# Lower parts of the weights all on VectorE, and attention units that follow their own columns of queries

## The chip, the cores and the metric

One core of a Trainium2 chip runs the program. The time is device microseconds of one execution; a time given for a kernel is the median of several. The engines are TensorE (PE; its weight loads PEld), VectorE (DVE), ScalarE (ACT), GpSimd (POOL) and SyncE (SP, which here only issues transfers).

## The reference

One decoder layer on 256 tokens of width 2048, all in float32, cut to what matters:

```python
xn = rms_norm(h, attn_norm_w)
nq, kcmp, vcmp, kslc, vslc, kwin, vwin, ngate, fq, fk, fv, ff = split(xn @ w_in)
# NSA, 16 heads in groups of 4 that share keys: three branches, gated
kc, vc = compress_blocks(kcmp), compress_blocks(vcmp)      # 15 blocks
p_cmp  = masked_softmax(nq @ kc * scale + bias_c)
o_nsa  = g0 * (p_cmp @ vc) + g1 * selected(nq, kslc, vslc) + g2 * window(nq, kwin, vwin)
# FoX, 16 heads: causal attention with a forgetting bias c[t] - c[s]
o_fox  = masked_softmax(fq @ fk * scale + c_t - c_s) @ fv
h = h + concat(rms_norm(o_nsa), rms_norm(o_fox)) @ w_out
# MoE: 4 groups x 8 experts, 2 of them for each token
h = h + sum_e combine[:, e] * ((silu(hn @ w_gate[e]) * (hn @ w_up[e])) @ w_down[e])
return rms_norm(h, final_norm_w)
```

With 256 tokens the selected and the window branch both see all causal keys.

## The kernel before

**Items.** The weights of w_in and w_out stream through SBUF in pieces of 1 MB, called items, in one fixed order. Items 0 to 3 are the compressed keys and values (kcv), 4 and 5 v0, 6 and 7 k0, 8 and 9 v1, 10 and 11 k1. The NSA queries come in four blocks of 256 columns, two items each: q00 (12, 13), q01 (14, 15), q10 (16, 17), q11 (18, 19); the first digit is the group G of 8 heads, the second the half i. FoX follows: fq00, fq01 (20 to 23), fk00 (24, 25), fv00 (26, 27), fk01 (28, 29), fv01 (30, 31), and the same for G = 1 in 32 to 43. Items 44 to 59 are w_out. `run_items` (L235) does an item: it issues a load three items ahead, converts the next item's two halves (`stream_conv`, L178), runs the matmuls, and calls `background` (L225) after each quarter. Items 4 to 43 have 8 pieces of 128 rows (nk = 8), the others 4.

**Conversion.** A float32 weight is split into an upper and a lower part. ScalarE copies the upper part (L191), then a subtraction makes the lower part (L192). For items of nk = 8 the first half's subtraction is on VectorE and the second half's on GpSimd (L189). The two halves rotate through three buffers (L185), so a half is converted when TensorE is done with the half three before it. A projection's matmuls use both parts, and the result is evacuated by ScalarE and VectorE (`end`, L320).

**Background work.** Each call of `background` moves on one step of the attention pipe (`attn_pipe`, L205) and one step of the generators in `misc` and in `splits`. The pipe takes four steps for a unit: step 1 computes scores and softmax of a new unit (`a`), step 2 transposes the probabilities of the one before it (`b`), step 4 multiplies that one by its values (`c`). So one item is one unit, and its `b` and `c` run in the next item. NSA has 16 units (`Tile`, L640): for a pair of heads first the tile of 256 keys (t = 1), then the one of 128 (t = 0), whose `c` ends the pair in `pair_end` (L572). There the compressed branch is added, by a matmul with `pTc[G]`. FoX has 8 units (`Unit`, L586), one for a pair of heads.

**Queries and the compressed part.** When a query block is done, `post_q` (L788) evacuates it into `scaled`, splits it into parts for the scores (`split_q`, L709: for i = 0 at once, for i = 1 in a step of `misc`), and appends `compressed(G, q, i)` (L730) to `misc`. That makes the scores with the compressed keys (csc), a softmax on VectorE and ScalarE with two clamps of 8 elements (L752, L758), and writes half of `pcm`. With i = 1, four steps later, it transposes `pcm` into the bank bpt (L772) and copies it to `pTc[G]`. The eight NSA units of a group are appended after its second block, so at items 15 and 19: they start in items 16 and 24, and the first FoX units in item 32.

**Banks.** csc, bpt, the scores (s_n, s_f) and the transposes (t_n, t_f) all take their PSUM bank from one tag `s` with three buffers in rotation (L96). A new one waits for the last reader of the one three before it.

**Other GpSimd work.** In the same stretch GpSimd adds the position parts for the compressed keys (bk, L500, eight additions in items 8 and 9, which the matmuls bhc need), the causal mask to the FoX bias (L822, L823, when a FoX bias is loaded) and the squares of the attention output (L580 to L584).

**Experts.** A ring of 20 slots holds expert weights. Two slots are loaded once 16 units are finished (L1116), others as w_out moves on (`at2`, L1137), and all later ones when the experts have used a slot.

Of the kernel before, what the change touches and what calls it, by code (L numbers as in the profile page):

```python
# [11 lines left out]
F32 = mybir.dt.float32  # L12
# [4 lines left out]
ALU = mybir.AluOpType  # L17
# [4 lines left out]
P = 128  # L22
T = 256
# [3 lines left out]
NBLK = 15  # L27
# [53 lines left out]
def tile_kernel(ctx: ExitStack, tc: tile.TileContext, a: dict, out):  # L81
    nc = tc.nc
    pe, act, dve, pool, sp = nc.tensor, nc.scalar, nc.vector, nc.gpsimd, nc.sync
# [12 lines left out]
    def bank(name, tag):  # L96
        return psa.tile([P, 512], F32, tag=tag, name=name, bufs=1 if tag == "o" else 3)
# [9 lines left out]
    with tc.using_default_side("right"):  # L107
        fp = rt_st.enter_context(tc.tile_pool(name="fp", bufs=1))
        wk = rt_st.enter_context(tc.tile_pool(name="wk", bufs=2))
        ap_q = rt_st.enter_context(tc.tile_pool(name="ap_q", bufs=2))  # L110

    def m8(tag, name, shape, dt=F32):
        return big.tile([P, *shape], dt, tag=tag, name=name)

    def mm(o, l, r, start, stop):
        pe.matmul(o, l, r, start=start, stop=stop, skip_group_check=True)  # L116
# [17 lines left out]
    ident = cst[:, K_ID:K_ID + P]  # L134
# [43 lines left out]
    def stream_conv(h):  # L178

        i, hf = divmod(h, 2)  # L180
        if i >= len(items):
            return
        nm, _, nk = items[i][:3]
        n2 = nk // 2
        cv = big.tile([P, n2, 2, 2048 // nk], F32R, tag=f"c{h % 3}", name=f"cv_{nm}_{hf}")  # L185
        hi, lo = cv[:, :, 0, :], cv[:, :, 1, :]
        r = raws[i][:, n2 * hf:n2 * hf + n2, :]
        n = n2 if h else n2 // 2
        eng = pool if hf and nk == 8 else dve  # L189
        for k in range(0, n2, n):  # L190
            act.activation(hi[:, k:k + n], r[:, k:k + n], AF.Copy)  # L191
            eng.tensor_tensor(lo[:, k:k + n], r[:, k:k + n], hi[:, k:k + n].bitcast(F32), ALU.subtract)  # L192
        halves[h] = cv

    def run_chunk(i, kk):
# [5 lines left out]
    misc, splits = deque(), deque()  # L201
# [33 lines left out]
    def run_items(lo_i, hi_i, after=None):  # L235
        for i in range(lo_i, hi_i):
            nk, post = items[i][2], items[i][4]
            stream_dma(i + DMA_AHEAD)
            for kk in range(nk):
                if kk % (nk // 2) == 0:  # L240
                    stream_conv(2 * i + 2 + 2 * kk // nk)
                run_chunk(i, kk)
                if (kk + 1) % (nk // 4) == 0:
                    background()
            if post is not None:
                post()
            if after is not None:
                after(i)
# [236 lines left out]
    vcbd = []  # L485
# [86 lines left out]
    def pair_end(i, oT):  # L572

        if i < 8:
            G, j = divmod(i, 4)
            mm(oT[:, :T], vcbd[0][:, G, j, :], pTc[G], False, True)
        act.copy(oraw[i // 8][:, i % 8, :], oT[:, :T])
        part = i // 8
        if i % 8 == 0:
            pool.tensor_tensor(sq[:, part, :], oraw[i // 8][:, i % 8, :], oraw[i // 8][:, i % 8, :], ALU.mult)  # L580
        else:
            s2 = wk.tile([P, T], F32, tag="s2", name=f"s2_{i}", bufs=1)
            pool.tensor_tensor(s2, oraw[i // 8][:, i % 8, :], oraw[i // 8][:, i % 8, :], ALU.mult)
            pool.tensor_tensor(sq[:, part, :], sq[:, part, :], s2, ALU.add)  # L584
# [121 lines left out]
    def evac_q(s_, q, i):  # L706
        row_scale(q[:, 2 * i:2 * i + 2, :], s_, 0.125)

    def split_q(s_, qs, j):  # L709

        act.copy(qs[0:64, j:j + 2, 0, :], s_[0:64, j:j + 2, :])
        dve.tensor_tensor(qs[64:128, j:j + 2, 0, :], s_[0:64, j:j + 2, :], qs[0:64, j:j + 2, 0, :].bitcast(F32),
                          ALU.subtract)
        u = qs[64:128, j:j + 2, 1, :]
        act.copy(u, s_[64:128, j:j + 2, :])
        act.copy(qs[0:64, j:j + 2, 1, :], u.bitcast(F32))
        dve.tensor_tensor(u, s_[64:128, j:j + 2, :], u.bitcast(F32), ALU.subtract)

    def split_q_later(q, qs):
        yield  # L720
        split_q(q, qs, 2)
        yield

    pTc = {}
    gb = gate.rearrange("p t (h b) -> p h t b", b=3)
    biases = {}

    pcms = {}

    def compressed(G, q, i):  # L730

        csc = bank(f"csc{G}{i}", "s")
        for t in range(2):
            for r in range(2):
                o0 = (t * 2 + r) * 32
                mm(csc[:, o0:o0 + 32], q[:, 2 * i + r, t * P:(t + 1) * P],
                   kcd[:, 2 * G + i].rearrange("p h c -> p (h c)"), t == 0 and r == 0, True)
        yield
        if i == 0:
            pcms[G] = wk.tile([P, 2, P], F32, tag="pcm", name=f"pcm{G}", bufs=1)  # L740
            pool.memset(pcms[G], 0.0)
        scs = wk.tile([P, 8, 16], F32, tag="scs", name=f"scs{G}{i}", bufs=2)
        mx = wk.tile([P, 8], F32, tag="mx", name=f"mx{G}{i}", bufs=2)
        ss = wk.tile([P, 8], F32, tag="ss", name=f"ss{G}{i}", bufs=2)
        scv = scs[:, :, 0:NBLK]
        for t in range(2):
            dve.tensor_tensor(scv[:, 4 * t:4 * t + 4],
                              csc[:, 64 * t:64 * t + 64].rearrange("p (u c) -> p u c", c=16)[:, :, 0:NBLK],
                              cb[:, t, 4 * G + 2 * i:4 * G + 2 * i + 2].rearrange("p r h c -> p (r h) c")[:, :, 0:NBLK],
                              ALU.add)  # L750
        dve.tensor_reduce(mx, scv, AX.X, ALU.max)
        dve.tensor_scalar(mx, mx, -1e29, None, ALU.max)  # L752
        dve.tensor_tensor(scv, scv, mx.unsqueeze(2).broadcast_to([P, 8, NBLK]), ALU.subtract)
        yield
        act.activation(scv, scv, AF.Exp)
        yield
        dve.tensor_reduce(ss, scv, AX.X, ALU.add)
        dve.tensor_scalar(ss, ss, 1e-30, None, ALU.max)  # L758
        dve.reciprocal(ss, ss)
        sst = ss.rearrange("p (t h) -> p t h", t=2)  # L760
        dve.tensor_tensor(sst, sst, gate.rearrange("p t (h b) -> p t h b", b=3)[:, :, 8 * G + 4 * i:8 * G + 4 * i + 4, 0],
                          ALU.mult)
        for t in range(2):
            dve.tensor_tensor(pcms[G][:, t, 64 * i:64 * i + 64].rearrange("p (h c) -> p h c", c=16)[:, :, 0:NBLK],
                              scv[:, 4 * t:4 * t + 4], sst[:, t].unsqueeze(2).broadcast_to([P, 4, NBLK]), ALU.mult)
        if i == 0:
            return
        for _ in range(4):
            yield
        bpt = bank(f"bpt{G}", "s")  # L770
        for t in range(2):
            pe.transpose(bpt[:, t * P:(t + 1) * P], pcms[G][:, t], ident)  # L772
        pt = fp.tile([P, T], F32, name=f"pTc{G}")
        act.copy(pt, bpt[:, :T])
        pTc[G] = pt
        yield

    def nsa_bias(g):
        if g not in biases:
            bias = ap_q.tile([P, 4, T], F32, tag="m6", name=f"bias{g}", bufs=2)  # L780
            act.dma_start(bias, bass.AP(tensor=rv_dr.tensor, offset=rv_dr.offset + 4 * g * 384,
                                        ap=[[1, P], [384, 4], [1, T]]))
            biases[g] = bias
        return biases[g]
# [3 lines left out]
    def post_q(s_, G, i):  # L788
        q = scaled
        evac_q(s_, q, i)  # L790
        if i == 0:
            qs2[G] = m8(f"m{2 + G}", f"q{G}", (4, 2, T), F32R)
            split_q(q, qs2[G], 0)
            misc.append(compressed(G, q, 0))
            return
        qs = qs2[G]
        misc.append(split_q_later(q, qs))
        misc.append(compressed(G, q, 1))
        for j in range(4):
            p = 4 * G + j  # L800
            g = p // 2
            pair = {"i": p}
            hs = [2 * (j % 2), 2 * (j % 2) + 1]

            for t in (1, 0):
                def bias_of(t=t, g=g, hs=hs, nxt=j % 2 == 1):
                    bi = nsa_bias(g)
                    if nxt:
                        nsa_bias(g + 1) if g < 3 else fox_bias(0)
                    return [bi[:, hh, t * P + P - 1::-1] for hh in hs]  # L810

                units.append(Tile(f"n{p}{t}", t, qs[:, j], g, bias_of,
                                  gate.rearrange("p t (h b) -> p t h b", b=3)[:, t, 2 * p:2 * p + 2, 1:3], pair))
# [68 lines left out]
    for G in range(2):  # L882
        for i in range(2):
            project(C_FQ + 512 * G + 256 * i, "T", f"fq{G}{i}", lambda s_, G=G, i=i: post_fq(s_, G, i))
        for hf in range(2):
            c = 512 * G + 256 * hf
# [196 lines left out]
    for i in range(4):  # L1083
# [3 lines left out]
        for kk in range(4):  # L1087
            k = 4 * i + kk
# [11 lines left out]
            if k in (5, 8, 11, 13):  # L1100
                n = (5, 8, 11, 13).index(k)
# [323 lines left out]
    for pr in range(16):  # L1425
        nm_ = str(pr)
        h = pr % 2
# [163 lines left out]
```

## Time and profile before

| | before |
|---|---|
| median of 3 runs | 1445.31 us (1440.64 to 1447.94) |
| the profiled execution | 1448.93 us |
| its span | 1447.1 us |
| TensorE busy | 1318.1 us, 91% |
| VectorE busy | 489.1 us, 34% |
| ScalarE busy | 326.8 us, 23% |
| GpSimd busy | 175.2 us, 12% |
| mean granted TensorE clock | 0.982 |

Busy shares are means over stages with different limits. Matmuls are pipelined and their ends are modelled, so a TensorE that is busy is not at its peak; its idle places and its granted clock tell more.

### The profile page before, as it was taken

Reading aid. Unit: us, or ns where it says so; the run is one execution under the profiler, and the core shown is the slowest. Engines: PE = TensorE matmul, PEld = TensorE weight load, DVE = VectorE, ACT = ScalarE, POOL = GpSimd, SP = SyncE. Lnnn points to the kernel's source line nnn. Section 1 sums busy time; section 2 is a strip of 40 time slices with the busy share of each in tenths; the row PEclk is TensorE's granted clock in tenths of the full one; section 3 lists DMA queues with packets and bytes.
Section 4 is the critical chain, followed back from the end, with each engine's and each line's share of the span. In section 5 each row is a group of like instructions: output and inputs, shape, how many; then the busy total and the mean of one; then the engine's idle time right before and its main releaser. Section 6 shows DMA issues by size and latency. Waiting matters only on the chain.

```text
span 1447.1 us, 17002 instructions
## 1 busy us (share of the span) xinstructions
PE 1318.1 (91%) x6822; PEld 739.9 (51%) x6822; DVE 489.1 (34%) x995; ACT 326.8 (23%) x655; POOL 175.2 (12%) x135
## 2 busy tenths in 40 slices
PE   9999799989999899999997997998899799799885
PEld 8778678877787633434433432433433243243332
DVE  4446676665766502222121220310301122031022
ACT  5435455644545200000000000000000000000003
POOL 0353233454200101100000000000000000000002
PEclk9999899999999999999999999999999999999998
DMA  8635335455487799999999999999999999999994
GB/s 269 204 118 160 119 116 169 161 175 160 130 337 260 275 382 421 405 422 420 421 421 421 421 421 421 421 420 421 421 421 422 420 421 421 421 421 421 421 403 165
DMA packets 128725, 479.95 MB, mean 332 GB/s; under 512 B 14112, under 2 KB 65152, under 8 KB 80384
## 3 DMA queue, kind: packets, MB, share of 16 engines
q1 hardware_dynamic: 124272, 474.53, 83.6%
q10 hardware_dynamic: 4368, 4.27, 0.9%
q8 instruction: 56, 0.92, 0.3%
q14 instruction: 29, 0.24, 0.0%
HBM read 476.63 MB, written 2.14 MB: 331 GB/s over the span
## 4 chain that ended last, share of the span: by engine, by line
DMA 42%; PE 42%; DVE 7%; ACT 4%; issue 2%; SPq 1%; POOL 1%; ACTq 0%; DVEq 0%; POOLq 0%
DMA e_u<-in_expert_w_up_dram 15%; DMA e_d<-in_expert_w_down_dram 15%; DMA e_g<-in_expert_w_gate_dram 11%; PE bu L116 7%; PE wo L116 6%; PE bg L116 5%; PE by L116 5%; PE fv_ps L116 3%; PE bx L116 2%; PE bo L116 2%; PE fk_ps L116 2%; PE q_ps L116 2%; PE o L116 2%; PE k_ps L116 1%; PE fq_ps L116 1%
## 5 line engine op out<-in xcount | busy, mean ns | idle before, releaser
L116 PE MATMUL by<-e_d,hids 128*64 128x512 f32 (+2 forms) x1072 | 234.6, 576 | 33.0 <-DMA e_d<-in_expert_w_down_dram 32.3
L116 PE MATMUL bu<-e_u,xg 128*64 128x512 f32 x1024 | 243.0, 597 | 8.6 <-DMA e_u<-in_expert_w_up_dram 8.6
L116 PE MATMUL bg<-e_g,xg 128*64 128x512 f32 x1024 | 235.4, 596 | 12.8 <-DMA e_g<-in_expert_w_gate_dram 12.8
L1375 DVE TENSOR_TENSOR ys<-by,ys 128x512 fp32r<-128x512 f32 x60 | 40.0, 687 | 455.7 <-ACT ys L1374 454.4
L116 PEld LDWEIGHTS by<-e_d,hids 128*64 128x64 f32 x1072 | 77.8, 137 | 182.6 <-issue 122.3
L116 PEld LDWEIGHTS bg<-e_g,xg 128*64 128x64 f32 x1024 | 80.3, 137 | 145.1 <-issue 111.4
L116 PEld LDWEIGHTS bu<-e_u,xg 128*64 128x64 f32 x1024 | 77.4, 136 | 144.5 <-issue 118.0
L1389 DVE TENSOR_TENSOR y<-y,bo 128x512 f32<-128x512 f32 x112 | 72.0, 684 | 150.7 <-PE bo L116 150.7
L1497 POOL TENSOR_TENSOR o<-y,e_fnw 128x256 f32<-128x256 f32 (+2 forms) x12 | 10.1, 865 | 836.0 <-DVE y L1410 836.0
L1374 ACT CAST ys<-by 128x512 fp32r<-128x512 f32 x60 | 35.2, 586 | 312.0 <-PE by L116 198.7
L116 PE MATMUL bo<-ys,scT 128*128 128x512 f32 x240 | 73.4, 426 | 13.4 <-ACT ys L1374 5.8
L116 PE MATMUL wo<-cv_wo,ohi 128*128 128x512 f32 x256 | 80.6, 396 | 0.0
L116 PEld LDWEIGHTS bx<-s,hh 128*128 128x128 f32 x512 | 64.1, 192 | 23.8 <-issue 13.0
L116 PE MATMUL bx<-s,hh 128*128 128x256 f32 x512 | 70.5, 291 | 4.6 <-DVE y L1389 2.9
L1303 DVE TENSOR_TENSOR xg<-bx,fw 128x512 f32<-128x512 f32 x64 | 43.5, 689 | 77.2 <-PE bx L116 77.2
L116 PEld LDWEIGHTS bo<-ys,scT 128*128 128x128 f32 x240 | 38.0, 188 | 60.1 <-issue 43.4
L116 PEld LDWEIGHTS wo<-cv_wo,ohi 128*128 128x128 f32 x256 | 46.9, 188 | 10.5 <-issue 1.2
L116 PE MATMUL fq_ps<-xhl,cv_fq 128*128 128x512 f32 (+1 forms) x256 | 52.1, 352 | 0.0
L116 PE MATMUL fk_ps<-xhl,cv_fk 128*128 128x512 f32 (+1 forms) x256 | 50.2, 347 | 0.0
L116 PE MATMUL wo<-cv_wo,olo 128*128 128x512 f32 x128 | 50.0, 390 | 0.0
L116 PE MATMUL q_ps<-xhl,cv_q 128*128 128x512 f32 (+1 forms) x256 | 49.9, 352 | 0.0
L1317 ACT CAST scT<-bsc 128x256 fp32r<-128x256 f32 x16 | 6.0, 372 | 194.2 <-PE bsc L116 194.2
(302 smaller groups left out, 1493.1 us busy)
## 6 DMA issues: line engine op xcount, KB each, us to landing
e_g<-in_expert_w_gate_dram SPq DMA_DIRECT2D x128, 1024.0 KB, 19.8
e_u<-in_expert_w_up_dram SPq DMA_DIRECT2D x128, 1024.0 KB, 19.8
e_d<-in_expert_w_down_dram SPq DMA_DIRECT2D x124, 1024.0 KB, 19.8
raw_wo<-in_w_out_dram SPq DMA_DIRECT2D x16, 1024.0 KB, 5.2
raw_q<-in_w_in_dram SPq DMA_DIRECT2D x8, 1024.0 KB, 5.4
raw_fq<-in_w_in_dram SPq DMA_DIRECT2D x8, 1024.0 KB, 5.2
raw_fk<-in_w_in_dram SPq DMA_DIRECT2D x8, 1024.0 KB, 5.2
raw_fv<-in_w_in_dram SPq DMA_DIRECT2D x8, 1024.0 KB, 5.2
```

The source lines that it names most:

```text
L116: pe.matmul(o, l, r, start=start, stop=stop, skip_group_check=True)
L1303: dve.tensor_tensor(xt_[:, i0:i0 + per, 0:m], bx.rearrange("p (i s) -> p i s", i=per), fw[:, 4 * j + i0:4 * j + i0 + per].unsqueeze(2).bro ...
L1317: act.copy(scT, bt[:, :T])
L1374: act.copy(hi, by[n])
L1375: dve.tensor_tensor(lo, by[n], hi.bitcast(F32), ALU.subtract)
L1389: dve.tensor_tensor(y[t][:, ns], base[t][:, ns], bo, ALU.add)
L1497: (dve if last else pool).tensor_tensor(o[t][:, ns], y[t][:, ns], fnw[:, ns], ALU.mult)
```

## The change

In `stream_conv` every lower part is made on VectorE. In `post_q` each half i of a group appends its own compressed part and its own four NSA units (pairs 2i and 2i + 1), so the first units of a group come after its first query block. `compressed` has a buffer `pcm` of its own for each half (one buffer in rotation, cleared by GpSimd each time), transposes it in each half, and stores `pTc[G, i]`; `pair_end` takes the one of its half. The NSA units so begin in item 14 instead of 16. The matmuls of `pair_end` stay the same in number; the rows of the other half in `pTc[G, i]` are zero.

```diff
@@ stream_conv
-        eng = pool if hf and nk == 8 else dve
         for k in range(0, n2, n):
             act.activation(hi[:, k:k + n], r[:, k:k + n], AF.Copy)
-            eng.tensor_tensor(lo[:, k:k + n], r[:, k:k + n], hi[:, k:k + n].bitcast(F32), ALU.subtract)
+            dve.tensor_tensor(lo[:, k:k + n], r[:, k:k + n], hi[:, k:k + n].bitcast(F32), ALU.subtract)
@@ pair_end
-            mm(oT[:, :T], vcbd[0][:, G, j, :], pTc[G], False, True)
+            mm(oT[:, :T], vcbd[0][:, G, j, :], pTc[G, j // 2], False, True)
@@ compressed
-        if i == 0:
-            pcms[G] = wk.tile([P, 2, P], F32, tag="pcm", name=f"pcm{G}", bufs=1)
-            pool.memset(pcms[G], 0.0)
+        pcm = wk.tile([P, 2, P], F32, tag="pcm", name=f"pcm{G}{i}", bufs=1)
+        pool.memset(pcm, 0.0)
...
-        if i == 0:
-            return
         for _ in range(4):
             yield
-        bpt = bank(f"bpt{G}", "s")
+        bpt = bank(f"bpt{G}{i}", "s")
         for t in range(2):
-            pe.transpose(bpt[:, t * P:(t + 1) * P], pcms[G][:, t], ident)
-        pt = fp.tile([P, T], F32, name=f"pTc{G}")
+            pe.transpose(bpt[:, t * P:(t + 1) * P], pcm[:, t], ident)
+        pt = fp.tile([P, T], F32, name=f"pTc{G}{i}")
         act.copy(pt, bpt[:, :T])
-        pTc[G] = pt
+        pTc[G, i] = pt
         yield
@@ post_q
         if i == 0:
             qs2[G] = m8(f"m{2 + G}", f"q{G}", (4, 2, T), F32R)
             split_q(q, qs2[G], 0)
-            misc.append(compressed(G, q, 0))
-            return
         qs = qs2[G]
-        misc.append(split_q_later(q, qs))
-        misc.append(compressed(G, q, 1))
-        for j in range(4):
+        if i:
+            misc.append(split_q_later(q, qs))
+        misc.append(compressed(G, q, i))
+        for j in (2 * i, 2 * i + 1):
```

## Rows read from the trace of the kernel before

**Rows 1.** The page, 40 slices of 36.2 us: what the DMA moved.

```profile
GB/s 269 204 118 160 119 116 169 161 175 160 130 337 260 275 382 421 405 422 420 421 421 421 421 421 421 421 420 421 421 421 422 420 421 421 421 421 421 421 403 165
```

**Rows 2.** The chain of waits in order of time: start us, us, what.

```profile
108.91 11.11 PE q_ps L116 x64
...
221.65 2.15 PE o L116 x18
...
237.71 2.08 PE o L116 x18
...
472.17 6.84 PE wo L116 x30
...
624.31 20.00 DMA e_d<-in_expert_w_down_dram
```

**Rows 3.** Timeline of TensorE: start, us, what, count, [idle before, releaser].

```profile
51.87 2.90 PE L116 MATMUL k_ps<-xhl,cv_k 128*128 128x512 f32 x8 [2.63 <-DVE kc L357]
...
83.69 0.43 PE L116 MATMUL bhc<-oraw,bk 128*64 128x128 f32 x2 [0.98 <-POOL bk L500]
86.42 1.97 PE L116 MATMUL bhc<-oraw,bk 128*64 128x128 f32 x14 [2.30 <-POOL bk L500]
...
122.13 1.08 PE L116 MATMUL csc<-kcd,scaled 128*128 128x32 f32 x8 [0.74 <-DVE scaled L359]
...
159.04 0.66 PE L772 MATMUL bpt<-cst,pcm 128*128 128x128 f32 x2 [7.37 <-DVE st_n L663]
...
200.68 0.41 PE L772 MATMUL bpt<-cst,pcm 128*128 128x128 f32 x2 [3.05 <-DVE st_n L663]
...
302.69 0.33 PE L626 MATMUL t_f<-cst,pr_f 128*128 128x128 f32 x1 [1.55 <-DVE st_f L610]
...
317.58 1.51 PE L116 MATMUL o<-pT_f,fox_m 128*64 128x256 f32 x8 [3.23 <-DVE pT_f L629]
...
362.28 1.55 PE L116 MATMUL o<-pT_f,fox_m 128*64 128x256 f32 x8 [2.73 <-DVE pT_f L629]
```

**Rows 4.** Busy us (count) of PE, PEld, DVE, ACT, POOL; granted clock, DMA, GB/s.

```profile
51.87:55.00 3.13, 3.13 (x11) 2.74 (x12) 1.21 (x2) 1.85 (x3) 0.00 (x0) 0.53 1.04 355
86.42:93.00 6.58, 6.58 (x39) 5.35 (x40) 0.00 (x0) 0.00 (x0) 2.25 (x1) 0.55 0.48 143
159.04:168.00 8.96, 8.96 (x38) 7.39 (x40) 3.39 (x16) 3.32 (x11) 2.36 (x1) 0.53 0.24 68
...
317.58:322.00 4.42, 4.42 (x19) 3.43 (x20) 1.99 (x3) 1.82 (x3) 1.35 (x2) 0.61 0.72 236
```

**Rows 5.** Line L192, one weight's lower parts: duration ns min/median/max, first and last start.

```profile
L192 DVE TENSOR_TENSOR cv_q<-raw_q,cv_q x8: 1217/1222/1228, 103.7 to 157.0; 128x1024 fp32r<-128x1024 f32 x8
L192 POOL TENSOR_TENSOR cv_q<-raw_q,cv_q x8: 2358/2406/2507, 106.6 to 162.4; 128x1024 fp32r<-128x1024 f32 x8
```

**Rows 6.** Timelines of VectorE and GpSimd around the FoX units.

```profile
298.65 3.43 DVE L192 TENSOR_TENSOR cv_fq<-raw_fq,cv_fq 128x1024 fp32r<-128x1024 f32 x1 [0.27 <-ACT cv_fq L191]
...
313.85 2.33 DVE L616 TENSOR_SCALAR sm_f<-sm_f 128x2 f32<-128x2 f32 x1
...
359.12 2.63 DVE L619 TENSOR_SCALAR pr_f<-pr_f,sm_f 128x256 f32<-128x256 f32 x2
...
313.80 2.35 POOL L192 TENSOR_TENSOR cv_fk<-raw_fk,cv_fk 128x1024 fp32r<-128x1024 f32 x1
```

**Rows 7.** Timeline of VectorE, evacuation of the compressed keys and values.

```profile
46.14 5.58 DVE L357 TENSOR_TENSOR kc<-kcv_ps,rsb 64x512 f32<-64x512 f32 x8
```

**Rows 8.** Timeline of VectorE in items 16 to 18.

```profile
136.30 0.42 DVE L663 CUSTOM_DVE_ANT_0 pr_n<-s_n,bias 128x256 f32<-128x256 f32 x1
...
139.49 1.14 DVE L672 TENSOR_SCALAR pr_n<-pr_n,sm_n 128x256 f32<-128x256 f32 x4
...
150.01 1.77 DVE L758 TENSOR_SCALAR ss<-ss 128x8 f32<-128x8 f32 x1
...
158.13 0.42 DVE L663 CUSTOM_DVE_ANT_0 pr_n<-s_n,bias 128x256 f32<-128x256 f32 x1
```

More of the change, by code (lines that the diff above doesn't have):

```diff
@@ L726, in tile_kernel @@
     biases = {}
-    pcms = {}
     def compressed(G, q, i):
@@ L763, in compressed @@
         for t in range(2):
-            dve.tensor_tensor(pcms[G][:, t, 64 * i:64 * i + 64].rearrange("p (h c) -> p h c", c=16)[:, :, 0:NBLK],
+            dve.tensor_tensor(pcm[:, t, 64 * i:64 * i + 64].rearrange("p (h c) -> p h c", c=16)[:, :, 0:NBLK],
                               scv[:, 4 * t:4 * t + 4], sst[:, t].unsqueeze(2).broadcast_to([P, 4, NBLK]), ALU.mult)
-        if i == 0:
-            return
         for _ in range(4):
             yield
-        bpt = bank(f"bpt{G}", "s")
+        bpt = bank(f"bpt{G}{i}", "s")
         for t in range(2):
-            pe.transpose(bpt[:, t * P:(t + 1) * P], pcms[G][:, t], ident)
-        pt = fp.tile([P, T], F32, name=f"pTc{G}")
+            pe.transpose(bpt[:, t * P:(t + 1) * P], pcm[:, t], ident)
+        pt = fp.tile([P, T], F32, name=f"pTc{G}{i}")
         act.copy(pt, bpt[:, :T])
-        pTc[G] = pt
+        pTc[G, i] = pt
         yield
```

## The prediction

> **What bounds the kernel now.** I read the page's slices first. From the fifteenth slice on (506 us) the DMA moves 382 to 422 GB/s until the last slice but one, and before that 116 to 337 [rows 1]: two stages with different limits. The chain of waits says the same: up to about 620 us it runs on TensorE (projections, then w_out), from 624 us on almost wholly on loads of expert weights [rows 2]. The edit lies wholly in the first stage, in the projection items 4 to 43. Slices thirteen and fourteen (434 to 506 us, 260 and 275 GB/s) are not saturated [rows 1], because the ring of weight slots is full and is freed by progress in w_out and the experts. So the saturated stream is tied to the place where the first stage ends, and a microsecond saved or lost before 470 us arrives at the end as one. I take 1:1; if the stream did not move, nothing would.
>
> Next the timeline of TensorE for the first stage, looking only at rows with an idle time in brackets [rows 3]. They are few and large: 2.63 us (k_ps, on kc), 0.98 and 2.30 (bhc, on GpSimd's bk), 0.74 (csc), 7.37 and 3.05 (bpt), 1.55 (t_f), 3.23 and 2.73 (o of FoX). Then the same engine's granted clock just behind them [rows 4]: it is 0.53 to 0.61 of full there, most of the stretch at 1.2 instead of 2.4 GHz. Length times the missing share is what each costs on top: 1.5 us behind kc, 3.0 behind bhc, 4.2 behind the first bpt, 1.7 behind the first o. The second bpt and the second o have idle times beside that o's (3.05 and 2.73 against 3.23), and I charge them the same 1.7. The 1.55 us wait shows in no such row and I charge none for it.
>
> **Part 1: the lower parts on VectorE.** One such subtraction takes 2.41 us on GpSimd and 1.22 us on VectorE [rows 5]. There are 40 (second half of items 4 to 43), so GpSimd loses 96 us and VectorE gains 49 us. Neither is the sum, since both engines have idle time; what counts is who waits.
>
> What the move gives back is seen where both engines work [rows 6]. A VectorE operation on 2 elements (L616) takes 2.33 us; it starts 0.05 us after a GpSimd subtraction and ends 0.03 us after it. A VectorE subtraction that takes 1.22 elsewhere takes 3.43 at 298.7 us, in the midst of GpSimd's work. VectorE was held until the other engine had finished. With the subtractions gone from GpSimd these holds vanish, except those by its other work (FoX bias, squares).
>
> Place by place:
>
> *kc (52 us), a loss.* The eight kc operations take 5.58 us on VectorE without a break [rows 7]. In the new order the second subtraction of item 5 sits between the fourth and the fifth. That is 1.2 us more wait for k_ps, 3.9 instead of 2.6. The wait nearest in size is bhc's 3.28, which cost 3.0 of clock against 1.5 here: 1.2 + up to 1.5. I take +2.0; bounds 0 and +2.7.
>
> *bhc (84 us), a gain.* TensorE waits for the eight bk additions on GpSimd. Ahead of them in GpSimd's queue stand two memsets and two subtractions of 2.41 us [rows 5]; the additions end where TensorE starts again, at 86.4 [rows 3]. Without the two subtractions of that stretch the queue still has to wait for what precedes the first memset, so I move the additions earlier by 2.4 to 4.0 us, and with kc's delay taken off the last one ends about 0.5 us after TensorE wants it. Gain 3.28 - 0.5 + 3.0 = 5.8; bounds 2 (one subtraction's 2.4 less the delay, clock unchanged) and 6.3.
>
> *FoX (300 to 362 us), a gain.* The t_f wait of 1.55 goes: the subtraction ahead of it no longer lasts 3.43. The first o waits 3.23 behind L616's 2.33; 2.16 of that goes, about 1.1 stays since the FoX bias still holds VectorE just before; with no clock loss (like the 1.55) that is 2.1 + 1.7 = 3.8. The second o waits 2.73 behind an L619 pair of 2.63 [rows 6]; held as L616 is, it gives back 2.1, and 1.7 of clock: 3.8. VectorE's new subtraction of those items is queued behind the copy (L629) that o waits for, so it does not take the gain back. Sum 9.2; bounds 4 (the other GpSimd work steps into the freed place and keeps the clock low) and 10.9 (all of it).
>
> **Part 2: units two items earlier.** The first four NSA units leave item 16 for item 14; the rest of the pipe follows, until the second group of FoX units (items 40 on) stands where it stood. Work in total is the same but for two more pairs of transposes, two more copies and two more memsets. A pair of transposes is 0.4 us (the second bpt, rows 3): +0.8 on TensorE; the memsets are on a GpSimd that then idles more.
>
> So the question is one of waits, in items 14 to 22. An item is 5.6 us of projection on TensorE (64 matmuls, 11.11 us, are two items, rows 2). What limits there is VectorE's backlog: the bpt transposes at 159 us write a bank that rotates among three, and it was last read by a unit's L663, which VectorE only begins at 158.13 [rows 8]. VectorE runs its queue in order: a unit of 256 keys occupies it from 136.30 to 140.63, 4.3 us including a wait for ScalarE's exponentials; then come the compressed part, with a clamp of 8 elements that lasts 1.77 us under a GpSimd hold [rows 8], and the query evacuations.
>
> I walked VectorE's queue and TensorE's by hand from 120.7 us on, in the new order, with the durations of these rows. VectorE gains one 1.22 subtraction an item and loses the clamp holds, about 1.4 us each, two to a compressed part: nearly even. TensorE first meets a new wait: at 121.4 the scores of the first unit need the split queries, which end at 124.7. It idles 2.9 us, where csc idles 0.74 now. Queued behind it are csc and the projection, but VectorE's backlog is later still, so this delay is absorbed. The walk puts the second compressed part's bpt (item 18, again right behind a unit of 256 keys, same collision of banks) at 166.0 with a wait of 5.9 us, against 7.37 at 159.0 now, with two units done more (4.9 us of TensorE work: two items with a unit of each kind last 16.06, from o to o, of which 11.11 is projection, rows 2). The next bpt (item 20) waits 0.5, the last (item 22, two steps behind its unit) nothing, against 3.05 now. Waits: 0.74 + 7.37 + 3.05 = 11.2 now; 2.9 + 0.8 (bank waits in item 16) + 5.9 + 0.5 = 10.1 then. Clock: 4.2 + 1.7 = 5.9 now; I take 2.4 behind the 5.9 wait, between the 3.0 and the 1.7 of the nearest rows. With the 0.8 of transposes the stretch goes from 17.1 to 13.3, so -4 rounded. Bounds: -12 (the item-18 wait and its clock gone as well) and +6 (the backlog walks 4 us later than mine and the clock stays low as long as now).
>
> One wait is new at the end: the third FoX unit now follows directly the evacuation that makes its keys, as csc follows the one it waits 0.74 for [rows 3]: +0.8, bounds 0.5 and 2.5 (with a clock loss like rows 4).
>
> Past item 31 the pipe idles two items longer. The two expert loads that depend on 16 finished units leave SP's queue two items earlier, at a time of 160 to 175 GB/s [rows 1]; they fill slots that then stay full, so nothing follows from it.
>
> **The sum.** +2.0 - 5.8 - 9.2 - 4 + 0.8 = -16.2 us. The profiled execution took 1448.9 (span 1447.1), 3.6 above the median of the runs, 1445.3; against the median this gives 1429.
>
> **Rivals.** *VectorE becomes the bound (slower).* Items 14 to 35 bring it 22 x 1.22 = 27 us. For two items with a pair of units TensorE takes 16.1 us [rows 2], and VectorE four subtractions (4.9), the unit of 256 keys (4.3), the smaller one (an estimate from it, 3.5), and a copy and evacuations (three of kc's 0.7, rows 7, 2.1): 14.8. It decides at about 0.7 us more an item: from there TensorE waits for each further microsecond. If every addition became a wait, less some 10 us of holds given back there, that is +17, and with the FoX and NSA gains lost and the early ones kept, 1445 + 17 - 4 = 1458. For it: VectorE's queue makes TensorE wait 7.37 at bpt now [rows 3]. Against it: that is one place with the compressed part; rows 3 hold no wait between 205 and 300 us. The Trainium skill's Perfetto Trace Analysis (Optimizing Scalar/DVE Operations) speaks for this rival: if DVE is saturated, offloading, even to GPSIMD, may make sense, so work should not come the other way; by it the time would be the 1458. It also warns that the two engines share a port and that exchange between them might not help; rows 6 show that sharing at work, and it favours the edit.
>
> *The NSA stall grows.* The walk is worst at item 18: if two units already in flight put 6 to 8 us more on the backlog and the clock falls as at 159 us, the stretch costs +4 to +6 instead of -4: 1437 to 1441.
>
> *Both stalls dissolve.* If VectorE without holds gains more than I count, the stretch gives 12: 1421, and with the bounds of the others 1416.
>
> *GpSimd is not what holds VectorE.* Then bhc still gains, FoX does not: 1438. Against it: both ends of the held operation coincide [rows 6].
>
> **How the numbers follow.** Forecast 0.62; VectorE bound 0.07; NSA stall 0.14; both dissolve 0.13; no hold 0.04. The forecast is 1429; the bounds of its terms put it between 1418 and 1440 in most mixtures. The range of 8 in 10 takes in most of the second and third rival: 1416 to 1442. A measurement of this kernel tells about 0.5% (7 us) from no change, that is 1438 to 1452.5. Faster: 0.60 of the forecast, 0.13, and 0.04 of the others, 0.77. Same: 0.16. Slower: 0.07.
>
> **What would show it.** In the changed profile: GpSimd's queue without L191/L192 work and bk done about when bhc starts, no half clock at 86 us; L616 and L619 at a fraction of a microsecond except beside the FoX bias; a bracket of 2 to 3 us at the first s_n, one of about 6 at the second bpt and none at the last; the expert stream starting some 16 us earlier. It is wrong if brackets on VectorE appear through items 23 to 33, if the second bpt waits over 10 us, or if the stage ends earlier and the end does not.

## The result, and the profile after

The changed kernel takes 1437.09 us (1436.08 to 1438.41), beside 1445.43 us of the kernel before in the same comparison: a ratio of 0.9943, 95% interval 0.9928 to 0.9958, that is 8.3 us less. 1429 was forecast, with a range of 1416 to 1442. The sign and the range hold. The number is that of the second rival (1437 to 1441).

| | before | after |
|---|---|---|
| the profiled execution, us | 1448.93 | 1436.38 |
| its span, us | 1447.1 | 1434.5 |
| first matmul of the experts (bx), us | 492.18 | 478.97 |
| GpSimd busy, us | 175.2 | 78.7 |
| VectorE busy, us | 489.1 | 509.1 |

The page of after, against [rows 1]: its span, busy times and the GB/s of 40 slices.

```profile
span 1434.5 us, 16952 instructions
...
PE 1312.0 (91%) x6826; PEld 734.4 (51%) x6826; DVE 509.1 (35%) x1035; ACT 328.0 (23%) x657; POOL 78.7 (5%) x97
...
GB/s 266 211 153 142 93 129 158 219 162 162 173 367 193 334 401 422 399 421 421 421 421 421 421 421 421 421 420 421 421 421 421 421 421 420 421 421 420 421 397 166
```

The stream of expert weights starts earlier and runs at the same 421 GB/s. The first bx comes 13.2 us earlier and the span is 12.6 us shorter, so a microsecond of the first stage was worth nearly one at the end. VectorE has 40 operations more (995 on the page of before, 1035 here), which at 1.22 us are 49 us, but it is busy only 20 us longer: the rest of its work got 29 us shorter.

TensorE's timeline of after, the rows that answer to [rows 3]: start, us, what, count, [idle before, releaser].

```profile
53.11 1.30 PE L116 MATMUL k_ps<-xhl,cv_k 128*128 128x512 f32 x3 [3.67 <-DVE kc L356]
...
84.09 1.09 PE L116 MATMUL bhc<-oraw,bk 128*64 128x128 f32 x16
...
118.68 0.73 PE L116 MATMUL s_n<-kT,q 128*128 128x512 f32 x2 [2.13 <-DVE q L711]
119.92 0.73 PE L116 MATMUL s_n<-kT,q 128*128 128x512 f32 x2 [0.51 <-DVE q L716]
...
160.18 0.66 PE L766 MATMUL bpt<-cst,pcm 128*128 128x128 f32 x2 [4.67 <-DVE st_n L662]
...
183.29 0.41 PE L766 MATMUL bpt<-cst,pcm 128*128 128x128 f32 x2 [1.68 <-DVE st_n L662]
...
284.10 0.92 PE L116 MATMUL s_f<-fox_m,fox_m 64*128 64x256 f32 x8 [1.30 <-DVE fox_m L356]
...
350.47 0.87 PE L116 MATMUL o<-pT_f,fox_m 128*64 128x256 f32 x8 [0.94 <-DVE pT_f L628]
```

The waits for bk, the t_f wait of 1.55 us and the first o wait of FoX are gone; the second o wait is 0.94 instead of 2.73. The kc wait has grown from 2.63 to 3.67. The waits in items 14 to 22 add up to 9.9 us (2.13, 0.51, 4.67, 1.68 and a t_n of 0.91), about the 10.1 that the walk gave. Next the granted clock behind the ones that remain, against [rows 4]: busy us (count) of PE, PEld, DVE, ACT, POOL; granted clock, DMA, GB/s.

```profile
53.11:56.64 3.53, 3.53 (x13) 3.14 (x14) 1.55 (x2) 1.85 (x3) 2.27 (x4) 0.52 1.06 337
...
121.50:124.90 3.40, 3.40 (x11) 2.82 (x11) 2.19 (x13) 2.90 (x9) 0.00 (x0) 0.50 0.00 0
...
160.18:169.28 9.10, 9.10 (x36) 7.49 (x38) 4.44 (x17) 3.31 (x11) 0.00 (x0) 0.50 0.35 112
169.28:200.00 30.72, 28.13 (x180) 23.99 (x177) 21.45 (x71) 17.93 (x44) 3.51 (x6) 1.00 0.28 88
```

TensorE is at 1.2 GHz for 9.1 us of work behind the second bpt, though that wait is 2.7 us shorter than the 7.37 of before; and it is at 1.2 GHz behind the first scores, where the prediction charged no clock. Work that takes a microsecond at half clock would take half of one at full clock, so it costs half a microsecond.

VectorE's timeline of after: the kc operations, the clamp L754, the queue ahead of the second bpt, FoX.

```profile
48.90 1.23 DVE L191 TENSOR_TENSOR cv_k<-raw_k,cv_k 128x1024 fp32r<-128x1024 f32 x1
...
151.53 0.17 DVE L754 TENSOR_SCALAR ss<-ss 128x8 f32<-128x8 f32 x1
...
155.75 0.68 DVE L711 TENSOR_TENSOR q<-scaled,q 64x512 fp32r<-64x512 f32 x1 [0.68 <-ACT q L710]
157.04 0.69 DVE L716 TENSOR_TENSOR q<-scaled,q 64x512 fp32r<-64x512 f32 x1 [0.60 <-ACT q L715]
158.12 1.23 DVE L191 TENSOR_TENSOR cv_q<-raw_q,cv_q 128x1024 fp32r<-128x1024 f32 x1 [0.39 <-ACT cv_q L190]
159.26 0.42 DVE L662 CUSTOM_DVE_ANT_0 pr_n<-s_n,bias 128x256 f32<-128x256 f32 x1
...
346.35 0.17 DVE L615 TENSOR_SCALAR sm_f<-sm_f 128x2 f32<-128x2 f32 x1 [0.29 <-ACT pr_f L611]
...
347.63 2.31 DVE L618 TENSOR_SCALAR pr_f<-pr_f,sm_f 128x256 f32<-128x256 f32 x2
```

The clamp that took 1.77 us [rows 8] takes 0.17. One pair in FoX (L618) still takes 2.31 us: GpSimd adds the mask to a FoX bias at that time, as the prediction said that its other work would. The three rows at 155 to 158 us become important below. GpSimd's timeline of after, the last of the bk additions:

```profile
53.04 2.09 POOL L499 TENSOR_TENSOR bk<-kc,vec 128x240 f32<-128x240 f32 x3 [0.28 <-DVE kc L356]
```

They end at 55.1 us, not at 86.4 [rows 3].

### The profile page after: what moved, and what is told of

It is laid out like the page before. It is cut to its first block, busy times and chain, and to the rows that moved or that the text cites. A ratio compares the mean times of both kernels' runs of the same rounds, so it can differ in the third digit from the quotient of the medians.

```text
span 1434.5 us, 16952 instructions
## 1 busy us (share of the span) xinstructions
PE 1312.0 (91%) x6826; PEld 734.4 (51%) x6826; DVE 509.1 (35%) x1035; ACT 328.0 (23%) x657; POOL 78.7 (5%) x97
## 4 chain that ended last, share of the span: by engine, by line
PE 44%; DMA 42%; DVE 7%; ACT 4%; issue 2%; SPq 1%; ACTq 0%; POOL 0%; DVEq 0%; POOLq 0%
DMA e_u<-in_expert_w_up_dram 16%; DMA e_d<-in_expert_w_down_dram 15%; DMA e_g<-in_expert_w_gate_dram 10%; PE bu L116 8%; PE wo L116 6%; PE bg L116 5%; PE by L116 5%; PE bx L116 2%; PE fv_ps L116 2%; PE bo L116 2%; PE fq_ps L116 2%; PE fk_ps L116 2%; PE k_ps L116 2%; PE o L116 2%; ACT pr_n L664 1%
## 5 line engine op out<-in xcount | busy, mean ns | idle before, releaser
L1490 POOL TENSOR_TENSOR o<-y,e_fnw 128x256 f32<-128x256 f32 (+2 forms) x12 | 10.1, 867 | 837.0 <-DVE y L1403 837.0
L116 PE MATMUL q_ps<-xhl,cv_q 128*128 128x512 f32 (+1 forms) x256 | 52.8, 362 | 0.0
L1347 ACT COPY hids<-bh 128x512 f32<-128x512 f32 x16 | 9.4, 585 | 182.2 <-PE bh L1345 182.2
L1336 ACT ACTIVATE hids<-bg,c 128x512 f32<-128x512 f32 x16 | 11.0, 687 | 169.9 <-PE bg L116 169.9
```

The costliest lines, as they stand in the source:

```text
L1336: act.activation(hids[-1], bg_, AF.Silu, scale=c2[:, 1:2])
L1347: act.copy(hT, bh.rearrange("p (i s) -> p i s", i=4))
L1490: (dve if last else pool).tensor_tensor(o[t][:, ns], y[t][:, ns], fnw[:, ns], ALU.mult)
```

## The experiments

One table reads all traces. It covers the stretch from 45 us to the first bx: TensorE's idle times over 0.25 us (the brackets of its timeline, added up), its busy time at 1.2 GHz (the stretches whose granted clock is 0.50), what both cost (idle plus half of the time at half clock), and the first bx. A filler is a matmul of constants that keeps TensorE busy; only those that a version adds are given in brackets. Times are those of the profiled execution of each kernel.

| kernel | idle | busy at half clock | cost | first bx |
|---|---|---|---|---|
| before | 32.73 | 27.35 | 46.4 | 492.18 |
| before, second trace | 32.43 | 20.33 | 42.6 | 488.69 |
| whole change | 24.77 | 15.93 | 32.7 | 478.97 |
| whole change, second trace | 24.72 | 18.80 | 34.1 | 479.32 |
| Part 1 alone | 23.12 | 12.81 | 29.5 | 474.99 |
| Part 1 alone, second trace | 23.38 | 9.14 | 28.0 | 473.44 |
| Part 2 alone | 34.87 | 19.19 | 44.5 | 491.60 |
| Part 1, dead subtractions on GpSimd | 34.52 | 19.14 | 44.1 | 489.39 |
| whole, filler ahead of the second bpt | 22.48 | 3.41 | 24.2 (+4.2 filler) | 474.61 |
| whole, later split | 21.40 | 10.07 | 26.4 | 472.01 |
| whole, other bank for bpt | 23.03 | 12.67 | 29.4 | 474.91 |
| whole, later split, two fillers, kc | 17.98 | 3.05 | 19.5 (+3.9) | 469.46 |
| Part 1, two fillers, kc | 14.41 | 0.00 | 14.4 (+7.9) | 467.43 |

First bx less the cost and the fillers is 445 to 447 us in every row. So these two quantities, idle time and time at half clock, account for what the kernels differ by, to within 2 us.

**Part 1 alone.**

```diff
-        eng = pool if hf and nk == 8 else dve
+        eng = dve
```

> Part 1 alone: all lower parts on VectorE, units and compressed part as before. Theory 'holds' (the gain comes from GpSimd no longer holding VectorE and no longer delaying bk): the wait of bhc and both waits of o are gone as in the changed kernel, k_ps waits about 3.7 us, the first bpt still waits 6 to 8 us with the clock low behind it; the whole comes to about the changed kernel's time, 1434 to 1440 us. Rival 'order' (the earlier units make the gain): less than half of it, over 1441 us.

Measured: 1431.84 us (1430.05 to 1435.37), ratio 0.9903 (0.9880 to 0.9926), which is better than the whole change and 2 us below what was expected. Its traces lack the wait for bk and the first o wait, and keep those of Part 2's place: TensorE waits 6.74 us at the first bpt. Part 1 was priced at 2.0 - 5.8 - 9.2 = -13.0; it gave -13.8.

**Part 2 alone.** The whole change, with the second halves on GpSimd as before.

```diff
-            dve.tensor_tensor(lo[:, k:k + n], ...)
+            (pool if hf and nk == 8 else dve).tensor_tensor(lo[:, k:k + n], ...)
```

> Part 2 alone: units and compressed part by half groups, the second halves' lower parts still on GpSimd. Theory 'holds': bhc still waits about 3.3 us with the clock low behind it, FoX units still wait, the first scores wait 2 to 3 us, the clamps of 8 elements still last 1.5 us and more; no gain, 1442 to 1452 us. Rival 'order': a gain of 5 us or more, 1440 us or less.

Measured: 1449.56 us (1446.45 to 1452.69), ratio 1.0026 (1.0010 to 1.0043): 3.9 us slower than 1445.63 of the same comparison. Three rows of its timelines, TensorE's first, then VectorE's:

```profile
123.48 0.72 PE L116 MATMUL s_n<-kT,q 128*128 128x512 f32 x2 [2.11 <-DVE q L711]
...
167.74 0.66 PE L766 MATMUL bpt<-cst,pcm 128*128 128x128 f32 x2 [6.99 <-DVE st_n L662]
```

```profile
150.56 2.02 DVE L748 TENSOR_SCALAR mx<-mx 128x8 f32<-128x8 f32 x1
...
158.63 1.78 DVE L754 TENSOR_SCALAR ss<-ss 128x8 f32<-128x8 f32 x1
```

The new wait at the first scores is there, five of the eight clamps of 8 elements are held beside GpSimd's subtractions (1.0 to 2.0 us; the other three take 0.17), and the wait at the second bpt is hardly shorter than the 7.37 of before.

**Both again on one chip.** Nothing is edited.

> The whole change again, unchanged, beside Part 1 alone on the same chip, for the price of Part 2 without a difference of jobs. Theory (Part 2 costs: the units that it brings ahead of the second bpt are paid at VectorE's price and given back at TensorE's): 4 to 5 us above Part 1 alone, 1437 against 1432. Rival (the difference between the two earlier jobs was chance): within 1.5 us of each other.

> Part 1 alone again, unchanged, beside the whole change on the same chip. Theory (Part 2 costs): 1431 to 1433, 4 to 5 us below the whole change. Its trace should show the waits of the first one within 0.3 us (3.7 at k_ps, 6.7 at the first bpt, 2.2 at the second, none at bhc, 0.9 at the second o), with stretches of half clock behind 52 and 149 us that may have other lengths. Rival (the difference between the two earlier jobs was chance): within 1.5 us of the whole change.

Measured: the whole change 1436.93 us (ratio 0.9937, 0.9917 to 0.9956), Part 1 alone 1430.37 us (ratio 0.9886, 0.9863 to 0.9909). Part 2 on top of Part 1 costs 6.6 us here, 5.2 between the two first runs, and 4.0 and 5.9 in the two pairs of first bx; 4 to 5 was expected. The difference was not chance. The waits of Part 1 came back within 0.1 us but for the second o of FoX (0.95 and 1.32), the clock did not. The first trace of Part 1 alone: TensorE's timeline at the first bpt, and the window behind it.

```profile
153.11 0.66 PE L772 MATMUL bpt<-cst,pcm 128*128 128x128 f32 x2 [6.74 <-DVE st_n L663]
```

```profile
153.11:162.51 9.40, 9.40 (x38) 7.71 (x40) 4.43 (x17) 3.31 (x11) 0.00 (x0) 0.50 0.36 112
```

The same two views of its second trace.

```profile
154.09 0.66 PE L772 MATMUL bpt<-cst,pcm 128*128 128x128 f32 x2 [6.68 <-DVE st_n L663]
```

```profile
154.09:157.47 3.38, 3.38 (x13) 2.99 (x13) 2.17 (x12) 3.31 (x11) 0.00 (x0) 0.50 0.00 0
```

The same wait in the same program is followed by 9.40 us of work at half clock in one execution and by 3.38 in another, 4.7 us lost against 1.7.

**The kernel before, a second trace.**

> The kernel before once more, for a second trace. Its profiled execution stood 3.5 us above the median of its runs. Theory (it is the length of the half clock behind the same waits that differs from run to run): the waits are those of the first trace within 0.3 us (2.6 at k_ps, 3.3 at bhc, 7.4 and 3.1 at bpt, 3.2 and 2.7 at o), but the stretches at half clock have other lengths, and their difference times one half is the difference of the spans up to the end of w_out within 1 us. Rival: the waits or the DMA differ, and the clock is the same (13.65 us behind the first bpt, 6.83 behind bhc, 3.41 behind four others).

Measured: 1445.16 us, span 1443.4, first bx 3.5 us earlier than in the first trace. TensorE's timeline at bpt, and the windows at half clock behind bhc, bpt and the second o:

```profile
158.24 0.66 PE L772 MATMUL bpt<-cst,pcm 128*128 128x128 f32 x2 [7.38 <-DVE st_n L663]
```

```profile
87.21:90.62 3.41, 3.41 (x17) 2.79 (x14) 0.00 (x0) 0.00 (x0) 1.81 (x1) 0.50 0.11 12
158.24:162.30 4.06, 4.06 (x16) 3.67 (x16) 2.20 (x11) 3.32 (x11) 0.67 (x1) 0.50 0.00 0
162.30:312.00 149.70, 141.75 (x912) 119.20 (x911) 104.26 (x322) 84.24 (x215) 68.61 (x45) 1.00 0.51 154
...
357.35:363.69 6.34, 6.34 (x23) 4.95 (x24) 1.92 (x2) 1.82 (x3) 1.35 (x2) 0.50 0.51 165
```

The waits are the same within 0.2 us (7.38 for 7.37, 3.05 again at the second bpt), the time at half clock is 20.33 instead of 27.35 us. Half of the difference is 3.5 us, as much as the first bx differs by; the spans differ by 3.7. Behind the second bpt (197.9 us) the clock does not fall at all, where the first trace had 3.4 us. So the theory holds: the trace that the prediction was made from was one with much time at half clock. Runs without a trace agree. Of the 17 runs of the kernel before that stand beside Part 1 alone, the seven under 1445 us have a mean granted clock of 0.986 to 0.988, the seven above 1448 us one of 0.981 to 0.986.

**Dead subtractions on GpSimd**, on Part 1 alone.

```diff
             eng.tensor_tensor(lo[:, k:k + n], r[:, k:k + n], hi[:, k:k + n].bitcast(F32), ALU.subtract)
+            if hf and nk == 8 and i >= 28:
+                pool.tensor_tensor(dead[:, 0:n], r[:, k:k + n], hi[:, k:k + n].bitcast(F32), ALU.subtract)
```

> Part 1 alone (VectorE makes all the lower parts), and in items 28 to 43 GpSimd also does the subtraction of each second half, as in the kernel before, but writes it to a tile that nobody reads. It is work added, on an engine that nobody waits for there. Theory (VectorE is held while GpSimd subtracts): the operations on two elements beside it (sm_f) take about 2.3 us again, the waits of TensorE at the first and second o of FoX come back (3.2 and 2.7 us, with half clock behind them of about 1.7 each), and of the 9.4 us that Part 1 saved in the FoX stretch most is gone: 1438 to 1442, against 1432 for Part 1 alone. Rival (Part 1 saves there because nothing waits for GpSimd's slower subtractions any more): no wait comes back, sm_f stays at about 0.2 us, 1431 to 1433.

Measured: 1448.29 us (1447.03 to 1452.04), 16 us above Part 1 alone and more than expected. TensorE at the first o of FoX, VectorE at an earlier pair and just before that o, and GpSimd:

```profile
305.46 0.87 PE L116 MATMUL o<-pT_f,fox_m 128*64 128x256 f32 x8 [2.65 <-DVE pT_f L632]
```

```profile
282.42 0.55 DVE L622 TENSOR_SCALAR pr_f<-pr_f,sm_f 128x256 f32<-128x256 f32 x2
...
302.21 2.64 DVE L622 TENSOR_SCALAR pr_f<-pr_f,sm_f 128x256 f32<-128x256 f32 x2
...
302.41 2.35 POOL L195 TENSOR_TENSOR dead<-raw_fq,cv_fq 128x1024 bf16<-128x1024 f32 x1 [0.86 <-POOL sq L583]
```

A pair that takes 0.55 us at 282.42 ends 0.09 us after the GpSimd operation that nobody waits for, and o waits 2.65 us. The hold is shown, and the rival (that the gain is only that of not waiting for GpSimd's product) falls. It fell on other instructions than I named: sm_f takes 1.0 us at most, as in Part 1 alone (1.1), while pr_f and the subtractions (up to 3.37 us for 1.22) are held. The loss is larger than the 9.4 us saved: from item 32 to the first bx it takes 216.2 us (203.7 in Part 1 alone, 213.1 before), and items 28 to 31 take 3.7 us more than in Part 1 alone. One reason is in the trace. VectorE's own subtraction of a second half, which in the kernel before GpSimd made, now runs beside the dead one of the same weight and is held by it: from 225 to 380 us VectorE's 33 subtractions add up to 53.2 us, in Part 1 alone to 44.3. Another is only argued: GpSimd reads the weight's tiles too, so they can come free later.

**A filler ahead of the second bpt**, on the whole change: 18 matmuls of constants (each is recorded as two, so x36), so that TensorE works while it waits.

```diff
+        if (G, i) == (0, 1):
+            keep_clock("clock2", 18)
         bpt = bank(f"bpt{G}{i}", "s")
```

> The changed kernel with 18 matmuls of 128x128 that compute nothing, into the output bank, right before the second bpt, so that TensorE works about 4 us of its 4.7 us wait. Theory 'clock' (the half clock behind that wait follows from TensorE's idleness): bpt starts where it did, within 0.5 us, the 9 us behind it run at full clock, the stage ends 4 to 5 us sooner, 1431 to 1434 us. Rival (the clock falls there for another reason, or the fill only delays bpt): 1436 us or more.

Measured: 1433.01 us (1429.54 to 1433.47), ratio 0.9908 (0.9886 to 0.9929). TensorE's timeline and the window around the filler:

```profile
153.89 4.18 PE L116 MATMUL clock<-onesq 128*128 128x128 f32 x36
159.72 0.41 PE L768 MATMUL bpt<-cst,pcm 128*128 128x128 f32 x2 [1.65 <-DVE st_n L662]
```

```profile
153.90:170.00 16.10, 14.45 (x111) 12.86 (x110) 10.92 (x34) 8.89 (x22) 1.60 (x3) 1.00 0.44 131
```

The clock stays at 2.4 GHz and the time falls by 4.1 us, close to the price of the 9.1 us at half clock (4.55). It is not the luck of one trace: the mean granted clock is 0.990 to 0.994 in the six runs, 0.986 to 0.990 in the ten of the whole change. This one trace has luck too, for the half clock behind the first scores, which lie ahead of the filler, is also missing. The end of the wait stays where it was (159.72 for 160.18), since VectorE decides it.

**A later split.** Group 1's first queries are split in a step of `misc`, like the other halves, and not at once in `post_q`.

```diff
-    def split_q_later(q, qs):
-        yield
-        split_q(q, qs, 2)
+    def split_q_later(q, qs, j):
+        yield
+        split_q(q, qs, j)
...
-            split_q(q, qs2[G], 0)
+            if G == 0:
+                split_q(q, qs2[G], 0)
...
-        if i:
-            misc.append(split_q_later(q, qs))
+        if i or G:
+            misc.append(split_q_later(q, qs, 2 * i))
```

> The changed kernel, but the split of the second group's first queries (item 17) is done two steps later from the background instead of at once. Theory 'backlog' (the second bpt waits because VectorE's queue, with this split and its waits for ScalarE in it, is late at the scores that hold the bank): its wait falls from 4.7 us by 2 to 2.7, the low clock behind it gets shorter, the kernel takes 1431 to 1435 us against 1437. Rival (the bank or ScalarE is late for another reason): wait and time as in the changed kernel, 1436 to 1439.

Measured: 1429.57 us (1427.64 to 1432.29), ratio 0.9886 (0.9862 to 0.9909), 7.5 us below the whole change and 1.4 below what was expected. VectorE's timeline ahead of the second bpt, then TensorE's at it:

```profile
155.73 1.22 DVE L191 TENSOR_TENSOR cv_q<-raw_q,cv_q 128x1024 fp32r<-128x1024 f32 x1
156.86 0.42 DVE L662 CUSTOM_DVE_ANT_0 pr_n<-s_n,bias 128x256 f32<-128x256 f32 x1
```

```profile
157.78 0.41 PE L766 MATMUL bpt<-cst,pcm 128*128 128x128 f32 x2 [1.52 <-DVE st_n L662]
```

The split's two operations and the 1.67 us in which VectorE waited for ScalarE between them (0.68, 0.60 and 0.39 in the rows of after) are out of the way. L662 starts at 156.86 instead of 159.26, 2.40 us earlier, and bpt is released 2.40 us earlier too. The wait falls by 3.15 us to 1.52, and no half clock follows it; the other 0.75 us of the fall come from TensorE, which arrives later in this trace, with 6.4 us of work at half clock behind the first scores instead of 3.4. So what ends this wait is VectorE's queue, and a good part of the queue was a split that nobody needed yet.

**Another bank for bpt**, on the whole change.

```diff
-        bpt = bank(f"bpt{G}{i}", "s")
+        bpt = bank(f"bpt{G}{i}", "o")
```

> The whole change, with one difference: the transposes bpt write the bank that otherwise takes the attention outputs o, instead of one of the three that rotate among scores, compressed scores and transposes. Nothing waits there for VectorE's reading of an older score bank any more. Theory (the collision of banks makes the wait): the waits of 4.67 and 1.68 us at the second and third bpt go, and with the first of them the half clock of 10.24 us behind it, worth about 4.5; the time falls from 1437 to 1427 to 1430. Rival (VectorE's backlog makes the wait, the bank only says where TensorE meets it): the wait comes back at the next matmul that needs VectorE, the t_n or the o of the same unit, with 2 us or more; only part of it and of the clock is saved, 1432 to 1436.

Measured: 1432.04 us (1429.81 to 1433.72), ratio 0.9894 (0.9871 to 0.9916). TensorE's timeline in the same place:

```profile
159.49 1.89 PE L116 MATMUL csc<-kcd,scaled 128*128 128x32 f32 x8 [3.16 <-DVE st_n L662]
```

bpt passes, and TensorE waits 3.16 us for the same reader at the next user of a rotating bank, csc, 0.7 us earlier than bpt was released (the first scores, too, come 0.7 us earlier in this trace). The rival is right in that the backlog sets the time and the bank only the place; it named t_n or o, and it was csc.

**Two versions with the leftovers filled.** On the later split: the kc subtraction back on GpSimd (`h == 13`), eight filler matmuls ahead of the first k_ps and eight ahead of the first s_n. On Part 1 alone: the same for kc and k_ps, and 26 filler matmuls ahead of the first bpt.

> The whole change with group 1's first queries split later, as in the run before it, and three small things: the one subtraction that stands among the kc operations (second half of item 6) goes back to GpSimd; eight matmuls of constants stand ahead of the first k_ps and eight ahead of the first s_n (about 1.9 us each), so that TensorE works in the two places where it still waits over 2 us. Theory (a wait costs its length and the half clock behind it, and a filler saves the clock only): kc wait 1.2 us shorter, 1.7 us of clock behind it and 1.7 to 3 behind the first s_n gone: 1424 to 1426, against 1429.6. Rival (the half clock does not depend on what TensorE did in the idle time): only the 1.2 us, 1428 to 1429.

> Part 1 alone with three small things: the subtraction among the kc operations stays on GpSimd, eight matmuls of constants stand ahead of the first k_ps, and 26 of them (6.0 us) ahead of the first bpt, whose wait of 6.7 us is the longest that Part 1 alone has. Theory (Part 2 is worth nothing once the half clock is filled): 1.2 us of kc wait, 1.7 of clock behind it and 4.7 of clock behind bpt go: 1424, no slower than the 1427 of the version that keeps Part 2. Rival (the clock was only a small part, or TensorE's own fillers run past VectorE): 1428 to 1431, and the version with Part 2 is the better one.

Measured: 1427.19 us (1426.81 to 1429.72), ratio 0.9864 (0.9846 to 0.9883), and 1425.99 us (1425.31 to 1426.83), ratio 0.9858 (0.9837 to 0.9879). The second, without Part 2, TensorE's timeline at the first bpt and two windows:

```profile
143.18 5.97 PE L116 MATMUL clock<-onesq 128*128 128x128 f32 x52
150.08 0.41 PE L776 MATMUL bpt<-cst,pcm 128*128 128x128 f32 x2 [0.94 <-DVE st_n L665]
```

```profile
40.00:160.00 120.00, 117.38 (x771) 101.58 (x770) 79.03 (x169) 60.53 (x103) 13.18 (x16) 1.00 0.55 167
160.00:465.00 305.00, 294.71 (x1726) 243.67 (x1725) 218.90 (x524) 166.75 (x354) 41.97 (x45) 1.00 0.59 196
```

Full clock from 40 to 465 us. This version is 20.7 us below the kernel before in its own comparison (1446.66), some 11 below the whole change and 2 above what was expected. The first version is 20.2 us below the kernel before in its own (1447.39), so the two are level within the noise; what they show is that Part 2 is not needed. In the first version the kc wait fell to 0.62 us and the next projection came 3.0 us earlier, as priced. The filler at the first s_n gave nothing: what TensorE gained there it waited at the second bpt, 2.52 us instead of 1.52 with 3.05 us at half clock behind. So the time was 1427, not 1424 to 1426.

## Why the prediction was right and where it failed

**Right: Part 1, term by term, its sum in part by luck.** The term kc, +2.0, was +1.0 in the wait and +0.8 to +2.2 by the next projection, clock included. The term bhc, -5.8, was -6.5, just past its bound of 6.3 (-5.4 against the second trace of before, with less half clock there). I let 0.5 us of wait remain, but with no subtraction ahead of them the bk additions ran at 47.6 to 55.1 us, 29 us before bhc, not 2.4 to 4.0 us earlier. What had held them in GpSimd's queue was the order behind subtractions of later weights. The term FoX, -9.2, was -9.4 and -9.2 in the two traces of Part 1 alone, from the first matmul of item 32 to the first bx. The mechanism, VectorE held by GpSimd, was shown by the dead subtractions. The sum -13.0 stands beside -13.8 and -16.3 between medians, but it comes so near to the first partly by luck. In the first traces Part 1 moves the first bx by 17.2 us: 14.7 in these three places and 2.5 in items 12 to 31, for which it had no term; against that, the trace of before stood 3.5 us above the median, as told below.

**Right: VectorE does not become the bound.** After 190 us no wait for VectorE in the projections is longer than the 1.30 us at the third FoX unit, which was priced at 0.8. From 169 to 200 us VectorE is busy 21.45 of 30.72 us. The Trainium skill's Perfetto Trace Analysis (Optimizing Scalar/DVE Operations) says that handing work even to GPSIMD may make sense if DVE is saturated, and warns that between these two, which share a port, it might not help. VectorE was busy 34% of the span before, and 17.31 us of the 20 from 180 to 200 us, so the runs hardly test the rule; the warning agrees with Part 1 alone, which took the work back to VectorE and gave 13.8 us.

**Wrong: Part 2's clock, the term "5.9 now; I take 2.4".** The walk of the queues had the waits nearly right: 2.9 + 0.8 + 5.9 + 0.5 = 10.1 against 2.64 + 4.67 + 1.68 + 0.91 = 9.9. But behind the second bpt 9.1 us of work ran at half clock, and 3.4 us behind the first scores, which the walk called absorbed: 6.25 us lost instead of 2.4. I took a price between two neighbours, as if it went with the length of the wait. The pairs of traces show that it does not: the same 6.7 us wait cost 4.7 and 1.7.

**Wrong: what Part 2 was compared with.** The -4 for the stretch was counted from the kernel before. Part 1 alone already shortens these waits, from 11.5 us (0.74, 7.37, 0.36, 3.05) to 9.7 (0.71, 6.74, 2.25), probably because the clamps are no longer held (0.17 us each but for one of 0.70), which no run tests by itself. On top of that Part 2 adds: 1.3 to 1.7 us of idle time and 1.6 to 4.8 us of clock in the table's two pairs. It pays at the first scores (2.64 us where csc waited 0.71) and at small new waits later, and it puts two more units into VectorE's queue ahead of the place where TensorE waits for that queue. That place is reached 7.1 us later (first L662 at 159.26, in Part 1 alone the same step at 152.19), close to the 7.8 us at which the prediction itself priced two units on VectorE; the units left out later give TensorE 6.0 us back (from item 32 to item 38: 42.3 instead of 48.3 us). The sign of Part 2 was wrong: priced at -3.2 with the third FoX unit's 0.8, it costs 4 to 7.

**Wrong: "against the median this gives 1429".** The profiled execution of before stood 3.5 us above the median of the comparison, and I took the terms from it whole. The second trace shows that the excess was the half clock itself (27.35 us of work against 20.33), so part of the 9.9 us of clock that the sum took away was not there in the median execution. After's profiled execution stands within 0.8 us of its median. Between profiled executions the change gave 12.6 us, between medians 8.3.

The sum, then. Of the 8 us between 1429 and 1437, 3.6 lie between the sum and the two profiled executions (16.2 against 12.6), nearly what the clock term of Part 2 was short by. The other 4.3 lie between these executions and the medians. Split by parts the miss is larger and cancels: by the first bx Part 1 gave 17.2 us instead of 13.0, and Part 2 on top of it cost 4.0 instead of giving 3.2. The second rival named the place (item 18) and the clock, but by a backlog 6 to 8 us longer than the walk's; the wait there was 4.67 us, not longer than the walk's 5.9.

## What to carry to other kernels

Price a step against the kernel in which the other steps are already done: the part that looked worth 3 us was worth less than nothing once the other had shortened the same waits. Moving work ahead of the place where one engine waits for another costs at the slow engine's price and comes back at the fast one's: here 7.1 against 6.0 us, the smaller part of what Part 2 cost, for the larger was half clock and the new wait at the first scores. Before a half clock is put into a sum as a gain, read a second trace of the same kernel; and where a wait can't be taken away, work that keeps TensorE busy takes the clock's part of it.

## What the runs showed of the hardware

- One engine can hold another without sharing its results: a VectorE pair of 0.55 us took 2.64 beside a GpSimd subtraction whose result nobody reads, and 40 subtractions moved from GpSimd (2.41 us each) to VectorE (1.22) made the kernel 13.8 us faster.
- The time at half clock behind one and the same wait differs from execution to execution: 9.40 and 3.38 us of work behind 6.7, 8.43 and 4.06 behind 7.4, 3.4 and none behind 3.05. In the projections, waits of 0.9 to 1.7 us had none behind them in the traces of the whole change.
- Matmuls of constants in the idle time kept the granted clock at 1.00: from 40 to 465 us without a break in Part 1 with two fillers, although TensorE still had idle times of up to 2.25 us there.
